# A batch-normalised matmul: one block's transposition moved from TensorE to the DMA, and the order of all tasks written down as a table

## The chip, the cores and the metric

The kernel runs on one core of a Trainium2 chip. The metric is the device time of one execution in microseconds (us), of which the median over runs is given. A trace of one profiled execution is used beside it. PE is TensorE, DVE is VectorE, ACT is ScalarE, POOL is GpSimd, SP is SyncE; on SP runs nothing but the issuing of DMAs.

## The reference

```python
y = np.matmul(x, weight)                 # x (16, 512, 1024), weight (1024, 768), float32
mean = np.mean(y, axis=(0, 1), keepdims=True)
var = np.var(y, axis=(0, 1), keepdims=True)
y_norm = (y - mean) / np.sqrt(var + eps)
return (gamma * y_norm + beta).astype(np.float32)
```

So y has 8192 rows and 768 columns, and every column is normalised over all 8192 rows. No output of a column can be written before the last row of that column has been multiplied.

## The kernel before

**Tiles.** The 768 columns are six column tiles `nt` of 128, the 8192 rows are sixteen chunks `c` of 512. x is loaded in bfloat16 by DMAs from GpSimd's queue, turned by VectorE so that the contraction lies on the partitions, and kept in SBUF. A unit of TensorE is one half of the contraction for one column tile and one chunk: four pairs of weight load and matmul with 512 moving columns (`col_unit`, line 575). Two such units fill one bank of PSUM; there are eight banks.

**Stages.** While x arrives, the first two column tiles are multiplied with rows on the partitions (line 510). Then column tiles 2, 3, 4 and 5 follow with columns on the partitions, so that a chunk's y is a block of 128 columns by 512 rows, transposed against the output. After each bank is full, VectorE takes its statistics (`bn`, line 711) and ScalarE copies it to SBUF as bfloat16 (`keep`, line 715); only then is the bank free. For column tile 2, ScalarE does both (lines 720 and 724). When a column tile is complete, `finish_tasks` makes its scale and shift.

**Output blocks.** Two chunks together are a block of 128 columns by 1024 rows (`col_block`). It is normalised in place (`norm`, lines 1023 and 1026) and must be transposed before it is stored. `MODE` on line 276 says how, for each block:

- `'xact'`: a transposing DMA on SP's queue (`xbar`, line 1220), then ScalarE's conversion to float32 (`convert`, line 1232), then the store (line 1202).
- `'pe'`: eight transpositions on TensorE into a PSUM bank (`turn_block`, line 1044), ScalarE's copy out of it (line 1210), then the store. The eight transpositions ride between the matmuls of later units, one after each matmul ("hosted").

Some blocks (`RAW`) are transposed by the DMA before they are normalised (line 1106), scaled by VectorE (line 1174) and shifted by GpSimd (line 1178); for these the scale and shift are spread over a PSUM tile by `raw_spread` (`turn` on lines 1141 and 1142, `gather` and `deal` on line 1145, on GpSimd or ScalarE, and ScalarE's copy on line 1158). The first two column tiles are normalised by VectorE (line 937) and shifted by GpSimd or VectorE (line 942).

**The end.** Column tile 5 is last. Two half blocks of column tile 4 are held back and copied out after the last matmul (line 1252). After the last statistics come ScalarE's square root (line 1311), three small instructions of VectorE (lines 1314, 1323, 1324), then norm (line 1348), transposition on TensorE (line 1044), ScalarE's copy (line 1361) and store (line 1364) for every block of the last column tile.

**The order.** Every step is a `Task` with a priority, an assumed duration and the tasks that it depends on. `arrange` goes through them in a planner's time, always takes the engine that can begin first and, on it, the task of lowest priority number among those that can begin within 0.2 us (`LOOK`); it also picks which TensorE unit hosts which transpositions and where buffers lie. Each engine then runs its instructions in exactly the order emitted, and waits on semaphores for what they need. VectorE tasks marked `lock` and GpSimd's arithmetic are not planned at the same time.

Of the kernel before, what the change touches and what calls it, by code (L numbers as in the profile page):

```python
# [97 lines left out]
class Wires:  # L98
# [8 lines left out]
    def ready(self, queue):  # L107
        lanes = self.lanes[queue]
        return 0.0 if len(lanes) < self.LANES else lanes[-self.LANES]
# [9 lines left out]
        return t, land  # L119


def arrange(tasks, turns, log=None):

    free = {e: 1.25 for e in ("PE", "DVE", "ACT", "POOL", "SP")}
    wires = Wires()
    port = {"DVE": 0.0, "POOL": 0.0}
    left = sorted(tasks, key=lambda t: t.prio)
    order = []  # L130
    SEM, LOOK = 0.06, 0.2

    def ready(t):
        if t.after is not None and t.after.end is None:
            return None
        r = 0.0
        for d in t.deps:
            if d.end is None:
                return None
            r = max(r, d.end + SEM + t.slack)  # L140
        kept = [(s.pool, s.pool.mark()) for s in t.takes] if len(t.takes) > 1 else []
        fits = True
        for s in t.takes:
            p = s.pool.place(s)
            if p is None:
                fits = False
                break
            r = max(r, p[0] + SEM)
            if kept:
                s.pool.take(s, p[1])  # L150
        for pool, mark in reversed(kept):
            pool.reset(mark)
        if not fits:
            return None
        if t.dma:
            r = max(r, wires.ready(list(t.engines)[0]))
        return r

    def start_of(t, r, e):

        b = max(r, free[e])
        if e == "DVE" and t.lock:
            b = max(b, port["POOL"])
        elif e == "POOL" and not t.dma:
            b = max(b, port["DVE"])
        return b

    while left:
        seen = [(t, ready(t)) for t in left]
        first = {}  # L170
        for t, r in seen:
            if r is not None:
                for e in t.engines:
                    b = start_of(t, r, e)
                    if e not in first or b < first[e]:
                        first[e] = b
        if not first:
            raise RuntimeError(f"nothing can begin: {[(t.prio, t.emit) for t in left[:8]]}")
        e = min(first, key=lambda k: first[k])
        best = None  # L180
        for t, r in seen:
            if r is not None and e in t.engines and start_of(t, r, e) <= first[e] + max(LOOK, t.look):
                if best is None or t.prio < best[1]:
                    best = start_of(t, r, e), t.prio, t
        start, _, t = best
        for s in t.takes:
            s.pool.take(s, s.pool.place(s)[1])
        occ, lat = t.engines[e]
        t.hosted = []
        if t.hosts:  # L190
            room = t.hosts
            for u, r in seen:
                if u in turns and r is not None and r <= start + 0.3 and room >= 1:
                    n = min(room, turns[u][0])
                    if turns[u][0] == turns[u][1]:
                        places = [s.pool.place(s) for s in u.takes]
                        if any(p is None or p[0] > start for p in places):
                            continue
                        for s in u.takes:
                            s.pool.take(s, s.pool.place(s)[1])  # L200
                        u.takes_done, u.takes = u.takes, []
                    t.hosted.append((u, n))
                    turns[u][0] -= n
                    room -= n
                    occ += 0.0555 * n
                    lat += 0.0555 * n
        if t in turns:
            occ = lat = 0.0555 * turns[t][0]
            lat += 0.2
            t.count = turns[t][0]  # L210
        free[e] = start + occ
        if e == "DVE" and t.lock or e == "POOL" and not t.dma:
            port[e] = start + occ
        t.end = start + lat
        if t.dma:
            free[e], t.end = wires.send(e, start, occ, t.dma, t.count)
        t.start, t.engine = start, e
        order.append(t)
        left.remove(t)
        for u, n in t.hosted:  # L220
            if turns[u][0] == 0:
                u.end = t.end + 0.2
                left.remove(u)
    return order


# [1 line left out]
def kernel(  # L228
# [9 lines left out]
    nc = tc.nc  # L238
# [3 lines left out]
    ALU = mybir.AluOpType  # L242
# [5 lines left out]
    P = 128  # L248
# [24 lines left out]
    XT, YB, SQ = C - EARLY, 28, 3  # L273
    ADDED = (0,6,16,28,40)
    PARTED, LATE, SINGLE = (4,5,7,8,9,10), (12,13,14,15), (2,3,6)
    MODE = {2:'xact',3:'xact',4:('pe',)*8}
    MODE = {nt: m if isinstance(m, tuple) else (m,) * (C // GY) for nt, m in MODE.items()}
    RAW, RAWADD, RAWDUE = {2:(0,2),3:(0,),4:(0,2,4)}, {2:'POOL',3:'POOL',4:'POOL'}, {2:14.0,3:8.0,4:8.0}
    RING = 3 * CH // 32 * KQ // 2
# [13 lines left out]
    def seq(bi):  # L293

        ins = bi.ins
        prev = last.get(ins.engine)
        if prev is not None:
            tc.add_manual_dep(
                ins, prev,
                mybir.DependencyInfo(mybir.DependencyClass.NoSync, mybir.DependencyReason.DATA),  # L300
                reason="order",
            )
        last[ins.engine] = ins.name
        return bi

    gamma_sb = singles.tile([P, NT], f32)
# [28 lines left out]
    ngamma = singles.tile([P, NT], f32)  # L335
# [29 lines left out]
    def act(occ):  # L365
        return {"ACT": (occ, occ + 0.11)}

    def pool(occ):
        return {"POOL": (occ, occ + 0.05)}
# [70 lines left out]
    order = [("x", 0), ("w", 0, 2), ("x", 1), ("w", 2, 4)]  # L440
# [5 lines left out]
    t = 1.0  # L446
    affine = None
# [237 lines left out]
    def y_of(nt, c):  # L685
        return y_col.setdefault((nt, c // GY), Slot(ys))
# [174 lines left out]
    S = clock[0]  # L861
# [61 lines left out]
    sr = task(U + 0.1, dve(0.35), shift_rows, [sc], True)  # L923
# [32 lines left out]
    k = 0  # L956
# [4 lines left out]


    def negate_gamma(eng):
        seq(nc.vector.tensor_scalar(ngamma, gamma_sb, -1.0, None, op0=ALU.mult))

    ng = task(S, dve(0.1), negate_gamma, [affine, sr], True)

    def finish_tasks(nt):
        deps = [col_end[nt, c][0] for c in range(C)]
# [49 lines left out]
    def norm(nt, c, n=1):  # L1019
        def emit(eng):  # L1020
            part = y(nt, c, n)
            if eng == "ACT":
                seq(nc.scalar.activation(
                    part, part, AF.Identity, bias=shift[:, nt:nt + 1], scale=scale[:, nt:nt + 1]))
            else:
                seq(nc.vector.tensor_scalar(
                    part, part, scale[:, nt:nt + 1], shift[:, nt:nt + 1],
                    op0=ALU.mult, op1=ALU.add))
        return emit
# [161 lines left out]
    def col_block(nt, c, due, fin_task, held=False):  # L1191
# [26 lines left out]
        def xbar(eng):  # L1218
# [49 lines left out]
    for nt in range(GA, NT - 1):  # L1268
# [10 lines left out]
        f = finish_tasks(nt)  # L1279
        start = clock[0] + 3.0  # L1280
# [58 lines left out]
    for c, r0, rows in ends:  # L1339
        due = E + 2.0 + 0.6 * c  # L1340
        n = max(rows // CH, 1)
# [13 lines left out]
        b, bank = turn_block(due + 0.6 * (n - 1), nt, m0, count, norms, [y_of(nt, c + i) for i in range(n)])  # L1355
# [7 lines left out]
        def store(eng, slot=slot, m0=m0, count=count):  # L1363
# [48 lines left out]
```

## Time and profile before

| What | Value |
|---|---|
| Median of 3 runs | 205.89 us (205.88 to 206.04) |
| Span of the profiled execution | 204.1 us (204.07) |
| What lies around the span, by the difference | 1.8 us |
| PE busy | 189.3 us, 93% |
| DVE, ACT, POOL busy | 159.3, 146.2, 124.1 us |
| Read from and written to HBM | 36.71 MB, 25.17 MB |

The profiled execution has no time of its own beside its span; the runs are 1.8 us longer than the span, and this difference is taken as constant. Busy time is counted between the first and the last instruction. A busy TensorE is not TensorE at its peak: matmuls are pipelined, and the mean of one instruction (371 ns for 512 columns) is longer than the distance from one to the next (0.216 us).

### The profile page before, as it was taken

How to read it: one execution, taken by the hardware profiler on the slowest of the kernel's cores; microseconds unless marked ns; L12 is line 12 of the kernel's file. 1: busy time of each engine (PE TensorE's matmuls, PEld its weight loads, DVE VectorE, ACT ScalarE, POOL GpSimd, SP SyncE). 2: the span in 40 equal slices, each digit the busy share in tenths (PEclk: the TensorE clock that was granted, in tenths of full speed). 3: DMA queues.
4: the chain of work that ended last, by engine and by line, in shares of the span. 5: the costliest groups of instructions: out<-in, count | busy, mean ns of one | idle time of the engine just before them, and what ended most of it. 6: DMA issues, size and time to landing. Idle time of an engine off the chain costs nothing.

```text
span 204.1 us, 3510 instructions
## 1 busy us (share of the span) xinstructions
PE 189.3 (93%) x1210; PEld 114.5 (56%) x1210; DVE 159.3 (78%) x250; ACT 146.2 (72%) x260; POOL 124.1 (61%) x150
## 2 busy tenths in 40 slices
PE   7969999999999999999999999999999999997900
PEld 3457554657488888777865444444444445544600
DVE  4031879999999999969989998987999878657900
ACT  2001461368989999899978766999998959956950
POOL 7776954877499989997403999389613312940000
PEclk9999999999999999999999999999999999999965
DMA  4999999999999999999686899899999999999998
GB/s 71 172 199 196 176 196 196 196 197 197 190 193 197 197 196 196 196 197 195 103 181 200 297 339 336 248 301 328 295 322 227 336 303 274 347 343 310 310 347 253
DMA packets 98562, 48.74 MB, mean 239 GB/s; under 512 B 24304, under 2 KB 98032, under 8 KB 98544
## 3 DMA queue, kind: packets, MB, share of 16 engines
q0 software_dynamic: 34624, 18.36, 65.5%
q1 hardware_dynamic: 63920, 30.16, 52.6%
q8 instruction: 9, 0.15, 0.3%
q14 instruction: 9, 0.07, 0.1%
HBM read 36.71 MB, written 25.17 MB: 303 GB/s over the span
## 4 chain that ended last, share of the span: by engine, by line
PE 86%; ACT 3%; DMA 3%; POOL 2%; issue 1%; ACTq 0%; DVE 0%; POOLq 0%
PE y_ps L575 54%; PE y_ps L510 24%; PE y_ps L814 4%; ACT o_sb L1361 3%; DMA ring<-in_x_dram 3%; PE o_ps L1044 1%; POOL ring L403 1%; POOL w_sb L387 1%; PE y_ps L753 1%; PE a_ps L903 1%; PE o_ps L1074 0%; ACTq L1407 0%; PE idle_ps L591 0%; PE tot_ps L871 0%; ACT ring L1252 0%
## 5 line engine op out<-in xcount | busy, mean ns | idle before, releaser
L575 PEld LDWEIGHTS <-w_sb 128*128 128x128 bf16 x520 | 50.3, 97 | 57.6
L575 PE MATMUL y_ps<-xT_sb,w_sb 128*128 128x512 bf16 (+1 forms) x272 | 59.3, 371 | 0.0
L575 PE MATMUL y_ps<-x_pl,w_sb 128*128 128x512 bf16 x248 | 57.4, 379 | 0.0
L403 POOL DMA_DIRECT2D ring<-in_x_dram x76 | 47.2, 626 | 14.4 <-DMA ring<-in_x_dram 5.5
L510 PE MATMUL y_ps<-w_sb,xT_sb 128*128 128x256 bf16 x448 | 50.6, 273 | 1.7 <-DMA ring<-in_x_dram 1.6
L510 PEld LDWEIGHTS <-xT_sb 128*128 128x128 bf16 x448 | 43.5, 98 | 9.4 <-DVE xT_sb L435 2.9
L435 DVE STREAM_TRANSPOSE xT_sb<-ring 128x1024 f32<-128x1024 f32 (+1 forms) x29 | 31.2, 1111 | 14.1 <-DMA ring<-in_x_dram 13.9
L711 DVE BATCH_NORM_STATS2 stats<-y_ps 128x6 f32<-128x512 f32 x46 | 30.9, 687 | 7.7 <-PE y_ps L575 7.2
L715 ACT CAST y_sb<-y_ps 128x512 bf16<-128x512 f32 x51 | 29.0, 593 | 10.4 <-DVE stats L711 6.3
L547 ACT COPY x_pl<-xT_sb 128x1024 bf16<-128x1024 bf16 x32 | 32.8, 1063 | 1.7 <-DVE xT_sb L435 1.7
L942 POOL TENSOR_TENSOR ring<-ring,sum 128x1024 f32<-128x1024 f32 (+1 forms) x11 | 23.8, 2188 | 14.9 <-ACT y_ps L724 10.9
L659 ACT ACTIVATE sq_sb<-y_ps 128x512 f32<-128x512 f32 x28 | 16.3, 610 | 16.2 <-PE y_ps L510 15.9
L666 POOL TENSOR_TENSOR sum<-sum,sq_sb 128x512 f32<-128x512 f32 x20 | 25.6, 1278 | 3.0 <-ACT sq_sb L659 1.7
L662 DVE TENSOR_TENSOR sum<-y_ps,sum 128x512 f32<-128x512 f32 x28 | 18.9, 675 | 6.3 <-ACT sq_sb L659 5.3
L672 ACT CAST y_sb<-y_ps 128x512 bf16<-128x512 f32 x28 | 16.3, 594 | 8.2 <-DVE sum L662 8.0
L1178 POOL TENSOR_TENSOR ring<-ring,sum 128x1024 f32<-128x1024 f32 x6 | 14.8, 2477 | 9.8 <-issue 8.5
L937 DVE TENSOR_TENSOR ring<-y_sb,a_ps 128x1024 f32<-128x1024 bf16 (+1 forms) x16 | 16.7, 1079 | 0.1
L1044 PE MATMUL o_ps<-ident,y_sb 128*128 128x128 bf16 x104 | 13.1, 221 | 1.6 <-DVE y_sb L1348 1.5
L1232 ACT CAST ring<-ring 128x1024 f32<-128x1024 bf16 x13 | 13.8, 1063 | 0.6 <-DMA ring<-y_sb 0.6
L1145 POOL COPY sum<-sum 32x256 f32<-32x256 f32 (+1 forms) x17 | 5.8, 340 | 13.4 <-DVE sum L1142 6.5
L428 DVE STREAM_TRANSPOSE xT_sb<-ring 128x2048 bf16<-128x2048 bf16 x6 | 13.5, 2290 | 0.1
L591 PE MATMUL idle_ps<-idle_sb 128*128 128x512 f32 x18 | 9.6, 688 | 1.5 <-DVE idle_sb L316 1.5
(104 smaller groups left out, 153.7 us busy)
## 6 DMA issues: line engine op xcount, KB each, us to landing
out_dram<-ring SPq DMA_DIRECT2D x37, 512.0 KB, 3.4
ring<-in_x_dram POOLq DMA_DIRECT2D x52, 256.0 KB, 8.8
out_dram<-o_sb SPq DMA_DIRECT2D x6, 512.0 KB, 4.7
ring<-in_x_dram POOLq DMA_DIRECT2D x16, 128.0 KB, 5.9
w_sb<-in_weight_dram POOLq DMA_DIRECT2D x8, 192.0 KB, 6.2
out_dram<-ring SPq DMA_DIRECT2D x6, 256.0 KB, 3.0
ring<-in_x_dram POOLq DMA_DIRECT2D x4, 192.0 KB, 7.8
out_dram<-o_sb SPq DMA_DIRECT2D x3, 256.0 KB, 2.5
```

Source lines behind the costliest of these rows:

```text
L403: bi = seq(nc.gpsimd.dma_start(x_bf[32 * i:32 * i + 32], src[:, :, KQ * i:KQ * (i + 1)]))
L435: seq(nc.vector.transpose(dst, src[:, :, jw0:jw1]))
L510: seq(nc.tensor.matmul(y_ps[:, s], x_of(c, jw, e, t * P, (t + 1) * P), w_sb[:, jw, e, 0:NA], start=(s == 0 and jw == 0 and e == 0), stop=( ...
L547: seq(nc.scalar.copy(dst, pairs) if eng == "ACT" else ENG[eng].tensor_copy(dst, pairs))
L575: seq(nc.tensor.matmul(y_ps, w_sb[:, jw, e, nt * P:(nt + 1) * P], moving(c, jw, e, q0 * QR, q1 * QR, parted), start=(jw == 0 and e == 0 an ...
L659: seq(nc.scalar.activation(sq_sb[:, 0:n], slot.tile[:, 0:n], AF.Square))
L662: seq(nc.vector.tensor_add(sum1, slot.tile[:, 0:n], sum1))
L666: seq(ENG[eng].tensor_add(acc, acc, state["sq"][:, 0:n]))
L711: seq(nc.vector.bn_stats(dst, slot.tile))
L715: seq(nc.scalar.copy(y(nt, c), slot.tile))
L937: seq(nc.vector.tensor_mul(slot.o, y_row[c].y[:, s0:s1], aff[0][:, None, :].to_broadcast([P, n, NA])))
L942: seq(ENG[eng].tensor_add(slot.o, slot.o, row[:, None, :].to_broadcast([P, n, NA])))
```

## The change

Three edits. `MODE` for column tile 4 gets `'xact'` for its fifth block (chunks 8 and 9) in place of `'pe'`. The negation of gamma goes from VectorE to GpSimd. And `arrange` no longer chooses: it walks a table, `ORDER`, of 783 words (786 tasks without the three that are wholly hosted), in which each word names the engine (P, V, A, G, S) and the number of the task in order of creation, and after a plus sign the hosted transpositions. The bookkeeping of times and buffers stays.

```diff
+ORDER = (
+    "G0 P59 G3 G8 A9 G4 G7 V1 V2 P60 G10 P61 P62 P63 P64 P65 V5 V6 P66 G12 P67 P68 P69 P70 P71 G14 P76 A72 "
...
+    "P637 P689 G546 V638 P677 P681 P690 P678 P673 P674 V641 S547 A642 A562 A631 A615 A639 V643 V691 V661 V644 "
+    "V657 V665 V669 V675 V679 S559 S569 S640 S563 G645 S662 G646 P682+666.1,658.3 P685+658.3,666.1 "
+    "P693+666.3,658.1 P686+658.1,666.2 P694+666.1 A692 A566 A570 A647 A663 A676 A680 V648 V687 V695 V683 S567 "
...
+    "A760 A770 S743 S766 S781 S776 S761 S785 S771 "
+)
-    left = sorted(tasks, key=lambda t: t.prio)
+    left = tasks
-    while left:
-        seen = [(t, ready(t)) for t in left]
-        ...
-        start, _, t = best
+    for word in ORDER.split():
+        word, _, riders = word.partition("+")
+        t, e = left[int(word[1:])], NAMES[word[0]]
+        r = ready(t)
+        if r is None:
+            raise RuntimeError(f"out of order: {word}")
+        start = start_of(t, r, e)
...
-    MODE = {2:'xact',3:'xact',4:('pe',)*8}
+    MODE = {2:'xact',3:'xact',4:('pe','pe','pe','pe','xact','pe','pe','pe')}
...
-        seq(nc.vector.tensor_scalar(ngamma, gamma_sb, -1.0, None, op0=ALU.mult))
-    ng = task(S, dve(0.1), negate_gamma, [affine, sr], True)
+        seq(nc.gpsimd.tensor_scalar(ngamma, gamma_sb, -1.0, None, op0=ALU.mult))
+    ng = task(S, pool(0.3), negate_gamma, [affine])
```

Built, the two programs issue the same instructions in the same order on every engine until the last two chunks of the first two column tiles are multiplied, about 95 us into the span. From there on the orders differ as follows.

- **TensorE**: the half units of column tiles 2 to 5 are shuffled among chunks, so that more banks are half full at a time. Eight transpositions are gone. Those of two blocks of column tile 4 (tasks 658 and 666) ride together, one to four to a unit, those of a third (670) in two portions later.
- **VectorE**: the table interleaves statistics, norms and copies otherwise; one of the sixteen copies of line 547 that both engines may do comes to it from ScalarE; the negation is gone. Of the first two column tiles' blocks, it begins with another half chunk (chunk 1 first).
- **ScalarE**: four of the six norms of column tile 2 follow one another directly. The third `gather` is gone from it. At the end the square root stands ahead of both held copies, and both are ahead of the first copy of the last column tile.
- **GpSimd**: the negation before its first line-942 task, and the third `gather`.
- **SP**: fourteen transposing DMAs of line 1220 in place of thirteen, three of column tiles 2 and 3 in a row at two places. At the end, the first piece stored has 256 rows, then come two of 512 and one of 1024 before the second one of 256; the last store is of 1024 rows and not of 512.

More of the change, by code (lines that the diff above doesn't have):

```diff
@@ L128, in arrange @@
     port = {"DVE": 0.0, "POOL": 0.0}
-    left = sorted(tasks, key=lambda t: t.prio)
+    left = tasks
     order = []
-    SEM, LOOK = 0.06, 0.2
+    SEM = 0.06
     def ready(t):
@@ L166, in start_of @@
         return b
-    while left:
-        seen = [(t, ready(t)) for t in left]
[L170 to L184, printed above, removed]
-        start, _, t = best
+    NAMES = {"P": "PE", "V": "DVE", "A": "ACT", "G": "POOL", "S": "SP"}
+    for word in ORDER.split():
[5 more added lines that the diff above has]
+        start = start_of(t, r, e)
         for s in t.takes:
@@ L189, in arrange @@
         t.hosted = []
[L190 to L206, printed above, removed]
+        for rider in riders.split(",") if riders else ():
+            i, n = rider.split(".")
+            u, n = left[int(i)], int(n)
+            if turns[u][0] == turns[u][1]:
+                for s in u.takes:
+                    s.pool.take(s, s.pool.place(s)[1])
+                u.takes_done, u.takes = u.takes, []
+            t.hosted.append((u, n))
+            turns[u][0] -= n
+            occ += 0.0555 * n
+            lat += 0.0555 * n
         if t in turns:
@@ L218, in arrange @@
         order.append(t)
-        left.remove(t)
         for u, n in t.hosted:
@@ L222, in arrange @@
                 u.end = t.end + 0.2
-                left.remove(u)
     return order
```

33 rows, old and new, of the table ORDER are left out of this document.

## The prediction

> **What bounds the kernel now.** First the page: busy time in slices, then the chain that ended last.
>
> ```profile
> PE   7969999999999999999999999999999999997900
> PEclk9999999999999999999999999999999999999965
> GB/s 71 172 199 196 176 196 196 196 197 197 190 193 197 197 196 196 196 197 195 103 181 200 297 339 336 248 301 328 295 322 227 336 303 274 347 343 310 310 347 253
> PE 86%; ACT 3%; DMA 3%; POOL 2%; issue 1%; ACTq 0%; DVE 0%; POOLq 0%
> ...
> 177.82 6.99 PE y_ps L575 x32
> 184.80 1.81 PE y_ps L753 x16
> ...
> 186.92 0.58 ACT ring L1252
> 187.51 0.20 ACT std L1311
> ...
> 188.59 0.54 PE o_ps L1044 x4
> ```
>
> TensorE has no gap from 25 us on until its last matmul ends at 184.80 + 1.81 = 186.62 us, at a full granted clock. No order can make it denser; only taking instructions away, or a new gap, moves that moment. After it the end is a chain of small steps, then output.
>
> Second, the DMA in stages, because the change adds a transfer (columns: window, its length, then busy time of PE, PEld, DVE, ACT, POOL, granted clock, DMA share, GB/s).
>
> ```profile
> 110.00:128.00 18.00, 18.00 (x88) 7.87 (x86) 16.89 (x20) 13.41 (x43) 16.72 (x8) 1.00 0.91 321
> 128.00:146.00 18.00, 18.00 (x84) 8.04 (x83) 15.89 (x23) 18.00 (x26) 14.00 (x12) 1.00 1.03 301
> 180.00:187.50 7.50, 7.06 (x47) 4.01 (x44) 4.36 (x11) 3.64 (x8) 2.05 (x1) 1.00 1.14 343
> 187.50:191.50 4.00, 2.87 (x33) 1.88 (x34) 3.76 (x14) 3.49 (x10) 0.00 (x0) 1.00 0.85 253
> 191.50:202.50 11.00, 2.59 (x33) 1.73 (x32) 2.14 (x7) 5.17 (x7) 0.00 (x0) 0.69 1.15 347
> 168.00:169.50 1.50, 1.50 (x10) 0.69 (x8) 1.47 (x7) 1.00 (x3) 0.00 (x0) 1.00 1.28 288
> ```
>
> The output goes at 347 GB/s when nothing else limits it, and it is at that rate for the last 11 us. It has one hole at the end: 4 us at 253 GB/s, worth 4 x (1 - 253/347) = 1.08 us. The last column tile is 8192 x 128 x 4 bytes = 4.19 MB, 12.1 us at 347 GB/s. So the end is: last matmul, 2.7 us to the first store (it is issued at 189.31 us), 12.1 us of output, and the landing.
>
> Third, what the moved block costs on each side.
>
> ```profile
> L1044 PE MATMUL o_ps<-ident,y_sb x56: 218/219/231, 169.2 to 190.0; 128*128 128x128 bf16 x56
> DMA to landing us min/median/max: 3.4/4.4/5.6
> L1232 ACT CAST ring<-ring 128x1024 f32<-128x1024 bf16 x13 | 13.8, 1063 | 0.6 <-DMA ring<-y_sb 0.6
> L1210 ACT CAST ring<-o_ps 128x1024 f32<-128x1024 bf16 x4 | 4.0, 1014 | 0.2 <-DMA out_dram<-ring 0.2
> 110.46 2.52 POOL L942 TENSOR_TENSOR ring<-ring,sum 128x512 f32<-128x512 f32 x2 [10.85 <-ACT y_ps L724]
> 131.19 4.70 POOL L942 TENSOR_TENSOR ring<-ring,sum 128x1024 f32<-128x1024 f32 x2 [3.54 <-DVE ring L937]
> ```
>
> The first is the transposition on TensorE, the second the time from issue to landing of the thirteen transposing DMAs of line 1220.
>
> **The change, part by part.** *Eight transpositions off TensorE.* A transposition lasts 219 ns but takes 0.06 us of the chain (it alternates with matmuls of 0.22 us there), so eight give 0.45 us: the last matmul ends at 186.17 us. ScalarE's part stays: 1.06 us for 1.01.
>
> *One transposing DMA more.* A block is 1024 x 128 x 2 bytes = 0.262 MB. In the window from 168.0 to 169.5 us, where transpositions fill the DMA, it moves 288 GB/s: 0.91 us. The upper bound is the median time of issue on SP, 1.70 us; the lower bound is the store rate, 0.76 us. I take 1.3, halfway between 0.91 and 1.70, because switching between stores and transpositions leaves dips. The Trainium skill has two figures, on "Advanced Engine Details and Errata", X-Bar Transpose (TRN2), that transposing DMAs run as fast as regular ones at 350 to 400 GB/s, and on "DMA: Bandwidth & Descriptors", Latency and other measured facts, 261 GB/s for a transposition that isn't contiguous. By the first the price would be an estimated 0.70 us, by the second 1.00; the trace's 288 GB/s lies between and nearer the second.
>
> This transfer falls at about 169 us. From 180 us on the DMA is at 343 of 347 GB/s, so it is not hidden beside anything there: it makes all later stores 1.3 us later, up to the hole at 187.5 us, which holds 1.08. If nothing else moved, the end would be 0.2 us later.
>
> *The order, early.* GpSimd starts its additions at 110.46 us, after VectorE's shift at 106.87 us and then two norms (0.73), the negation (0.16), a product (0.68), an addition (0.69), two norms (0.73), a product (0.68). In the table stand three norms (1.1) and one product (0.68): GpSimd can start at about 108.7, 1.8 us sooner, and its later wait of 3.54 us on line 937 shrinks too. The output of the first two column tiles then comes sooner, in stages that ran at 321 and 301 GB/s; the lead, up to 1.8 us, pays for the 1.3 of the transposition. The negation on GpSimd lies in its 10.85 us of idle time: nothing. The third gather costs ScalarE 1.00 us less and GpSimd about 0.9 more, off the path unless GpSimd's addition behind it is late.
>
> *The order, the end.* ScalarE's square root starts when the statistics are aggregated in both. But now both held copies (0.58 each) and both keeps (0.37) stand between it and the first output copy; before, one held copy was done ahead of it. Root 186.97, then at starting distances of about 0.5, 0.3, 0.5 and 0.3 us the first output copy starts at 188.75 in place of 188.91 - 0.45 = 188.46: it loses 0.28 us. Then come pieces of 256, 512, 512 and 1024 rows instead of 256, 256, 512 and 512. Two pieces of 0.131 MB took 0.88 us on SP, 298 GB/s, under the DMA's rate, so one of them less, and more queued behind it, closes part of the hole: between 0 and 1.08 us, I take 0.3, the lower part, since half of the hole lies before the first store.
>
> Sum against the profiled span of 204.07 us: -0.45 + 0.28 - 0.30 = -0.47, with the transposition paid by the early lead. With 1.82 us around the span as before, 205.89 - 0.47 = **205.4 us**.
>
> **The rivals.** *(1) TensorE runs into full banks.* This is the mechanism for a slower end. Before, in program order, a bank was used again 10.45 us (six units of 1.73) after its last matmul in most of column tiles 3 to 5. In the table many gaps are 2.6 to 5 us, and a drain takes 0.69 (statistics) + 0.59 (keep) and semaphores, 1.4 us at best, and waits for whatever stands ahead in ScalarE's queue. The tightest place is column tile 5: a bank with a `'pe'` block's transpositions is full at 174.5 us and wanted again at 177.2, if I count the table's units on from 109 us with 0.216 us a matmul (0.226 where a row's step is two). Ahead of its copy, ScalarE has the conversion of the new block (0.95), two keeps (0.5 each) and another block's copy (0.93); with its own 0.93 that is 3.8 us. The new block's norm ends at 168.55 (it stands behind statistics of a unit that ends at 167.4). With the median landing of 4.4 us the conversion begins at 173.0 and the bank is free at 176.8: 0.4 us to spare. From a landing of 4.8 us on TensorE waits, at the largest landing seen, 5.6, for 0.8 us; and VectorE waited up to 0.72 us for a store to free its buffer, which the old order hid. About eight places have 0.1 to 1.3 us to spare, and a stall at one gives slack to the next, so the largest counts: 0.8 to 2 us, time 206.2 to 207.4, say 206.9. For it: every conversion now stands close ahead of keeps. Against: laid out with the rows' durations, no place is late by itself.
>
> *(2) The DMA stays the bound.* If the early lead is lost (three transpositions in a row on SP, stores behind them), the 1.3 us remain, up to 1.70 and more with a pause: 0.2 to 0.6 us later than before, 206.2. For it: 343 GB/s before the end. Against: 2 us of room at 301 to 321 GB/s earlier.
>
> *(3) Nothing to see.* The gain of TensorE is eaten by ScalarE's order at the end: -0.45 + 0.28, 205.7. This is part of the forecast's own range, 205.1 to 205.8.
>
> **How the numbers follow.** What a measurement of this kernel can tell from no change is about 0.2%, 0.41 us. My case has a chance of 0.50, of which 0.37 lie below 205.48 and 0.13 within 0.2% (the forecast stands only just outside). Rival 1 has 0.37, all slower. Rival 2 has 0.13, 0.05 within 0.2% and 0.08 slower. That makes faster 0.37, same 0.18, slower 0.45. The range for 8 in 10 goes from 204.9 (the whole hole closed) to 207.1, leaving out the worst of rival 1.
>
> **What would show it.** Right: TensorE without gaps up to a last matmul at about 186.2 us; GpSimd's first line-942 task near 108.7; a first output store at about 189.1; more than 253 GB/s in the four us after 187.5. Wrong: waits of TensorE on ScalarE in lines 1210, 1232 or 715, as the waits of PE name them, above all between 125 and 145 and between 170 and 178 us (rival 1); a last matmul in time but 347 GB/s without a hole from 180 us to a later end (rival 2); conversions on ScalarE that wait for a landing longer than 4.8 us.

## The result, and the profile after

| | before | changed |
|---|---|---|
| Median of six runs | 205.94 us (205.65 to 206.11) | 206.93 us (206.64 to 207.98) |
| Ratio, 95% interval | | 1.0055 (1.0039 to 1.0071) |
| Span of the profiled execution | 204.07 us | 204.99 us |

The changed kernel is slower by about 1.0 us. Every line of the changed kernel stands 24 lines lower than before (575 is 599, 1044 is 1068, 1364 is 1388).

The page first: TensorE's and the clock's slices, the DMA's rate, the shares of the chain that ended last.

```profile
PE   7989999999999999999999999999999999996830
PEclk9999999999999999999999999999999999999575
GB/s 71 159 201 196 194 196 196 196 197 196 190 194 197 196 196 197 196 197 194 95 202 170 381 357 308 234 355 337 310 229 338 221 292 329 332 343 293 343 347 184
PE 79%; DMA 9%; DVE 3%; POOL 2%; ACT 1%; issue 1%; ACTq 0%; DVEq 0%; POOLq 0%
```

Two rows of the chain itself (start, length, engine, tile, line):

```profile
184.52 1.83 PE y_ps L777 x16
...
187.12 0.30 ACT std L1335
```

From 95 us on, where the orders begin to differ, TensorE has no new gap (ahead of that it stood for 0.13 us at 18.4 and 0.27 us at 25.8 us, waiting for data; the old order with six gamma loads, below, shows 0.28 us at 26.0 in the same place). Its last matmul ends at 184.52 + 1.83 = 186.35 us, 0.27 us sooner than before. So the loss lies behind it, or beside it. The DMA in stages (the columns as before, GB/s last):

```profile
110.00:128.00 18.00, 17.89 (x80) 7.79 (x81) 17.21 (x20) 15.07 (x50) 16.52 (x9) 1.00 0.97 342
128.00:146.00 18.00, 17.94 (x82) 8.02 (x83) 14.76 (x23) 15.43 (x21) 13.42 (x12) 1.00 1.12 308
146.00:165.00 19.00, 18.89 (x87) 8.51 (x88) 17.25 (x35) 16.61 (x25) 5.68 (x8) 1.00 1.10 271
165.00:180.00 15.00, 14.88 (x86) 7.42 (x87) 10.30 (x21) 11.85 (x18) 5.68 (x9) 1.00 1.17 322
180.00:187.50 7.50, 6.78 (x46) 3.96 (x44) 6.35 (x15) 4.53 (x9) 4.09 (x2) 1.00 1.13 340
187.50:191.50 4.00, 2.80 (x28) 1.90 (x28) 3.93 (x14) 3.86 (x9) 0.00 (x0) 0.83 0.93 281
191.50:202.50 11.00, 4.23 (x37) 3.67 (x36) 1.84 (x6) 5.36 (x6) 0.00 (x0) 0.66 1.15 347
```

The early stages run faster than before (342 for 321, 308 for 301), the hole before the end is smaller (281 for 253), and yet the end is later. From 146 to 165 us the rate is lower than before. The two stages of the kernel before that the prediction doesn't show:

```profile
146.00:165.00 19.00, 19.00 (x89) 8.58 (x88) 17.08 (x34) 16.47 (x25) 5.19 (x9) 1.00 1.19 288
165.00:180.00 15.00, 15.00 (x95) 7.73 (x93) 11.99 (x24) 13.11 (x22) 6.37 (x6) 1.00 1.12 320
```

The lead on GpSimd, the first output copy on ScalarE and the first output store on SP, from their timelines:

```profile
108.84 12.05 POOL L966 TENSOR_TENSOR ring<-ring,sum 128x512 f32<-128x512 f32 x6 [8.87 <-DVE ring L961]
```

```profile
188.79 2.57 ACT L1385 CAST o_sb<-o_ps 128x256 f32<-128x256 bf16 x5
```

```profile
189.22 10.15 SPq L1388 DMA_DIRECT2D out_dram<-o_sb  x11
```

**Three pieces make up the loss.** (1) The trace holds sixteen completion events for each store, which I read as one from each of the 16 DMA engines. In both kernels the last of the sixteen falls behind the other 15 after 180 us, and from then on the last completions of the stores follow one another at the time of their transfers (about 1.51 us for 512 KB, 0.76 for 256 KB, 0.38 for 128 KB) up to the end: that engine has no pause. From the completion events:

| | first output store issued | 15 engines done | last engine done |
|---|---|---|---|
| before | 189.31 | 203.13 | 203.15 |
| changed | 189.22 | 203.00 | 203.54 |

The 15 gained 0.13 us; the last landing is 0.39 later. Both figures contain 0.14 us that came from the start of this execution and not from the change: the last matmul of the first two column tiles, up to which the orders are the same, ended at 94.86 us in place of 94.72. Counted from that moment the profiles agree far better:

| us from the end of that matmul | last matmul | first output store | 15 engines done | last engine done |
|---|---|---|---|---|
| before | 91.90 | 94.60 | 108.41 | 108.44 |
| before, six loads (below) | 91.90 | 94.60 | 108.42 | 108.54 |
| changed | 91.47 | 94.36 | 108.15 | 108.68 |
| changed, four loads (below) | 91.47 | 94.36 | 108.15 | 108.64 |

So by the order TensorE is 0.43 us sooner, the 15 engines 0.27 sooner and the last engine 0.25 us later than in the first row.

(2) After it the program waits on SP for eight completion semaphores, one after another. The instructions of the program's last line from 203.1 us on (count, shortest, median and longest in ns, first and last start), before and changed:

```profile
L1407 SPq EVENT_SEMAPHORE  x3: 17/17/28, 203.2 to 204.0; - x3
...
L1407 ACTq DRAIN  x1: 14/14/14, 203.5 to 203.5; - x1
```

```profile
L1431 SPq EVENT_SEMAPHORE  x10: 17/28/28, 203.6 to 204.9; - x10
...
L1431 ACTq DRAIN  x1: 142/142/142, 204.6 to 204.6; - x1
```

Two of these belong to the last steps in both; so one wait came behind the last landing before, and eight do now, 0.06 us each: 0.43 us. SP's waits show the same from the other side (total, times, longest): before, SP still waited for landings three times, the longest 1.5 us; now it waits once for 4.1 us, on the first semaphore, and finds the other seven done.

```profile
SPq L1407 <- DMA out_dram<-o_sb: 2.8, 3, 1.5
```

```profile
SPq L1431 <- DMA out_dram<-o_sb: 4.1, 1, 4.1
```

(3) ScalarE's DRAIN takes 142 ns in place of 14, comes late and makes the last steps 0.10 us longer. It does so in every kernel below that has the whole table or all but its last entries, and in no other. In just these kernels an 8 KB packet of instructions stands 0.3 us behind the end of the span (205.30 us here), and in the others the last one comes before 192 us; whether that is the cause was not tried. 0.39 + 0.43 + 0.10 = 0.92 us, the difference of the spans, of which 0.14 is the start of the execution.

### The profile page after: what moved, and what is told of

The parts are those of the page before. It is cut to its first block, busy times and chain, and to the rows that moved or that the text cites. A ratio compares the mean times of both kernels' runs of the same rounds, so it can differ in the third digit from the quotient of the medians.

```text
span 205.0 us, 3478 instructions
## 1 busy us (share of the span) xinstructions
PE 190.3 (93%) x1188; PEld 116.2 (57%) x1202; DVE 158.9 (78%) x250; ACT 143.2 (70%) x255; POOL 126.9 (62%) x155
## 4 chain that ended last, share of the span: by engine, by line
PE 79%; DMA 9%; DVE 3%; POOL 2%; ACT 1%; issue 1%; ACTq 0%; DVEq 0%; POOLq 0%
PE y_ps L599 50%; PE y_ps L534 21%; DMA w_sb<-in_weight_dram 6%; PE y_ps L838 4%; DMA ring<-in_x_dram 3%; DVE y_sb L1372 2%; PE o_ps L1068 2%; ACT o_sb L1385 1%; POOL ring L427 1%; PE y_ps L777 1%; POOL w_sb L411 1%; DVE xT_sb L459 1%; PE a_ps L927 1%; PE o_ps L1098 0%; ACTq L1431 0%
## 5 line engine op out<-in xcount | busy, mean ns | idle before, releaser
L599 PE MATMUL y_ps<-xT_sb,w_sb 128*128 128x512 bf16 (+1 forms) x265 | 60.2, 371 | 0.3
L459 DVE STREAM_TRANSPOSE xT_sb<-ring 128x1024 f32<-128x1024 f32 (+1 forms) x29 | 31.3, 1112 | 13.8 <-DMA ring<-in_x_dram 13.6
L739 ACT CAST y_sb<-y_ps 128x512 bf16<-128x512 f32 x51 | 28.0, 589 | 10.3 <-DVE stats L735 7.7
L735 DVE BATCH_NORM_STATS2 stats<-y_ps 128x6 f32<-128x512 f32 x46 | 30.0, 685 | 6.4 <-PE y_ps L599 6.4
L571 ACT COPY x_pl<-xT_sb 128x1024 bf16<-128x1024 bf16 x31 | 31.8, 1053 | 1.7 <-DVE xT_sb L459 1.7
L696 ACT CAST y_sb<-y_ps 128x512 bf16<-128x512 f32 x28 | 16.0, 602 | 7.6 <-DVE sum L686 7.4
L1202 POOL TENSOR_TENSOR ring<-ring,sum 128x1024 f32<-128x1024 f32 x6 | 14.1, 2366 | 9.2 <-issue 5.6
L1169 POOL COPY sum<-sum 32x64 f32<-32x64 f32 (+1 forms) x21 | 8.6, 412 | 15.2 <-DVE sum L1166 14.4
L1256 ACT CAST ring<-ring 128x1024 f32<-128x1024 bf16 x14 | 14.4, 1045 | 0.5 <-DMA ring<-y_sb 0.4
L615 PE MATMUL idle_ps<-idle_sb 128*128 128x512 f32 x18 | 10.3, 727 | 1.5 <-DVE idle_sb L340 1.5
```

The costliest lines, as they stand in the source:

```text
L459: seq(nc.vector.transpose(dst, src[:, :, jw0:jw1]))
L571: seq(nc.scalar.copy(dst, pairs) if eng == "ACT" else ENG[eng].tensor_copy(dst, pairs))
L599: seq(nc.tensor.matmul(y_ps, w_sb[:, jw, e, nt * P:(nt + 1) * P], moving(c, jw, e, q0 * QR, q1 * QR, parted), start=(jw == 0 and e == 0 an ...
L735: seq(nc.vector.bn_stats(dst, slot.tile))
L739: seq(nc.scalar.copy(y(nt, c), slot.tile))
```

## The experiments

All ratios are to the kernel before on the same chip, with 95% intervals. What the expectations call a ring is one of the 16 DMA engines.

### The waits at the end

One gamma load less in the changed kernel, so that SP issues 88 DMAs again and not 89:

```diff
-    PAIRED = 1
+    PAIRED = 2
```

> The changed kernel with one DMA issue less on SP: gamma comes in four loads instead of five (two columns a load for the first four column tiles), 88 issues instead of 89, everything else as it is. Theory of the last waits: at the end SP waits for eight completion semaphores one after another in a fixed order at 0.06 us each, and with 89 issues the last store is on the first of the eight, so seven more waits follow its landing than before; with 88 the last store is on the last of the eight again, one wait follows, and the time falls by 7 x 0.06 = 0.43 us, to about 206.5 us, ratio to before 1.003. Theory that the whole loss is DMA work (one more transposition, a ring that lags): a load of 1 KB at the start changes nothing, 206.9 us, ratio 1.0055.

206.34 us, ratio 1.0029 (1.0012 to 1.0047): 0.6 us better than the changed kernel. The ten semaphore instructions at the end are three again:

```profile
L1431 SPq EVENT_SEMAPHORE  x3: 17/17/28, 203.8 to 204.7; - x3
...
L1431 ACTq DRAIN  x1: 141/141/141, 204.4 to 204.4; - x1
```

And one load more in the kernel before:

```diff
-    PAIRED = 1
+    PAIRED = 0
```

> The kernel before with one DMA issue more on SP: six gamma loads instead of five, 89 issues instead of 88, nothing else. Theory of the last waits: the last store moves to the semaphore that is waited for first, seven waits of 0.06 us come behind its landing, 0.43 us slower than before, ratio 1.002. Theory that the number of issues doesn't matter: ratio 1.000.

206.26 us, ratio 1.0029 (1.0014 to 1.0044), with the ten waits of the changed kernel:

```profile
L1407 SPq EVENT_SEMAPHORE  x10: 17/28/28, 203.6 to 204.9; - x10
```

Both directions agree, at sizes that hold 0.43 us. The number of DMA issues decides which of the eight semaphores the last store is on; one transposition more moved it from the last to the first. The late DRAIN of ScalarE stays with four loads: it goes with the table, not with the count.

### The transposition and the table

The kernel before, planned by itself, with the block moved:

```diff
-    MODE = {2:'xact',3:'xact',4:('pe',)*8}
+    MODE = {2:'xact',3:'xact',4:('pe','pe','pe','pe','xact','pe','pe','pe')}
-    PAIRED = 1
+    PAIRED = 2
```

> The kernel before, in its own planned order, with the one block of the fifth column tile turned by the DMA, and with four gamma loads so that the issues stay 88; no table, and the negation on VectorE. Theory that the transposition is what is paid for (0.91 to 1.3 us of DMA in a stage with no room): slower than before by 0.3 us or more, or no faster although the last matmul ends 0.3 to 0.45 us sooner. Theory that the table is at fault and the transposition is a gain: 0.3 us faster than before, ratio 0.9985 or less.

207.42 us, ratio 1.0075 (1.0059 to 1.0091): 1.5 us slower than before, with a last matmul at 186.36 us. The hole is gone:

```profile
187.50:191.50 4.00, 3.12 (x31) 2.62 (x32) 3.93 (x14) 3.28 (x7) 0.00 (x0) 0.76 1.14 341
```

So the transposition without the table costs 1.5 us, and the table gives 1.1 of it back (206.34 with the same count of issues). Which part of the table? The order of before up to about 153 us, and the new table's order from there:

```diff
-ORDER = "(the table's 783 words)"
+ORDER = "(610 words: the order of before, written out) (what is left of the table's words, in its order)"
-    PAIRED = 1
+    PAIRED = 2
```

> The other half: the order of the kernel before up to about 153 us (its first 610 tasks, the negation on VectorE), from there the table's order with the transposing DMA; four gamma loads, 88 issues. Theory that the table's early lead pays for the transposition: without it the loss of the planned order with the block moved comes back, ratio near 1.0075 (207.4 us). Theory that the table's late order is what helps (fewer stores that find the DMA empty at the end, three transpositions behind one another): ratio near that of the changed kernel with four gamma loads, 1.003 (206.3 us).

207.59 us, ratio 1.0081 (1.0060 to 1.0103): without the early lead the whole loss is back. The early part of the table is what pays. (The two orders fit less than perfectly here too: TensorE's last matmul came 92.40 us after those of the first two column tiles and not 91.47. But the end is later than this alone allows: first output store at 190.53 us, and 13.8 us behind it, by the bound found below, is 204.3; the last engine was done at 205.02.) Is the transposing DMA itself then still felt in the changed kernel?

```diff
-            seq(nc.sync.dma_start_transpose(t_slot.o, y(nt, c, GY)))
+            if nt != 4:
+                seq(nc.sync.dma_start_transpose(t_slot.o, y(nt, c, GY)))
...
-                seq(nc.scalar.copy(slot.o, t_slot.o))
+                src = t_slot.o if nt != 4 else y(nt, c, GY).rearrange("p (s n) -> p s n", n=P)
+                seq(nc.scalar.copy(slot.o, src))
```

> The changed kernel without its new transposing DMA: the conversion on ScalarE reads the block as VectorE wrote it, so that this block's output is not turned; TensorE doesn't turn it either; 88 issues with five gamma loads. What the DMA costs in the changed kernel, everything else as it is: compared with the changed kernel with four gamma loads (206.34 us, also 88 issues). Theory that the DMA bounds the end and the transposition is 0.91 to 1.3 us of it: faster by 0.4 to 1.0 us (the rest is hidden once the hole before the end opens again), 205.3 to 205.9 us, ratio to before 0.997 to 1.000. Theory that the early lead hides it wholly: no change, 206.3 us, ratio 1.002 to 1.003.

The kernel leaves this one block unturned. 206.47 us, ratio 1.0034 (1.0013 to 1.0055), no better than with it (1.0029). From 165 to 180 us the DMA moves 308 GB/s in place of 320: without the transfer it isn't filled. Last, the other half, with the block on TensorE:

```diff
-ORDER = "(the table's 783 words)"
+ORDER = "(the table's first 610 words) (what is left, in the order of before)"
-    MODE = {2:'xact',3:'xact',4:('pe','pe','pe','pe','xact','pe','pe','pe')}
+    MODE = {2:'xact',3:'xact',4:('pe',)*8}
```

> The table's order up to about 155 us (its first 610 entries), from there the order of the kernel before, written out as a table; the block stays on TensorE (no transposing DMA more, 88 issues). Theory that the table's early lead only pays for the transposition's DMA work: without that transposition the DMA has room anyway (hole of 1.08 us before the end), TensorE's last matmul and the first output store set the end as before, so the time is that of before, ratio 0.999 to 1.001. Theory that the early lead is worth something by itself: about 1.1 us faster than before, as the table is against the planned order with the block moved (206.34 against 207.42), ratio 0.995. Theory that the early part of the table is a loss: slower than 1.002.

209.77 us, ratio 1.0191 (1.0171 to 1.0210), slower by far more than any theory said. At the seam the two orders do not fit: a transposition (line 1127 there) stands on SP in front of stores that are ready, and waits 7.4 us for its input.

```profile
SPq L1127 <- ACT y_sb L736: 7.4, 1, 7.4
```

This run says nothing on what the lead is worth without the transposition. That stays open.

### The order at the end

Four loads, and the last words of the table (from its 713th) in the order of before:

```diff
-ORDER = "(the table's 783 words)"
+ORDER = "(the table's first 712 words) (what is left, in the order of before)"
```

> The changed kernel with four gamma loads whose last 71 entries stand in the order of the kernel before: output pieces of 256, 256, 512 and 512 rows, the second held copy and the second keep later on ScalarE. By the prediction's terms the old order wins 0.28 us for the first output copy and loses 0.3 us in the hole: no change within 0.1 us, 206.3 us, ratio 1.003. If the DMA alone bounds the end: no change either, but with an earlier first store (188.9 in place of 189.2 us). If the new order of the end is itself a loss: 0.3 us faster, ratio 1.0015; if it is a gain that was hidden: 0.3 us slower or more, ratio 1.0045.

206.51 us, ratio 1.0045 (1.0024 to 1.0065). The first store came at 189.64 us, not sooner: in the spliced order a keep and a held copy stood ahead of ScalarE's square root, which began at 187.72 us (187.37 with four loads alone). The lagging engine was then only 0.20 us behind at the end. The ratio is the one of the last theory, but against four loads alone (1.0029) it is no gain and no loss beyond the intervals: the run decides for none of them.

Four loads, and the second keep (A719) behind the first output copy (A738):

```diff
-A734 A719 S732 ... V772 V782 V778 ... P737 P745 ... A738 A746
+A734 S732 ... V772 P737 A738 A719 V782 V778 ... P745 ... A746
```

> The changed kernel with four gamma loads, and ScalarE's second keep of the last column piece (0.39 us, between the second held copy and the first output copy) moved behind the first output copy; nothing else. Theory that the first output store sets the end: it comes 0.17 to 0.28 us sooner (at about 0.3 us behind TensorE's transposition as before) and the time falls by as much, about 206.1 us, ratio 1.0015 to 1.002. Theory that the DMA ring that is behind by the instruction fetch sets the end (it has no idle time from 181.5 us on): an earlier first store with the same end, 206.3 us, ratio 1.003.

206.32 us, ratio 1.0019 (1.0007 to 1.0030); with four loads alone it was 206.34. From the last matmul to the first store it took 2.79 us in place of 2.87: the other work of the end left only 0.08 us to win, and one engine was still 0.52 us behind the 15 at the last landing. By the ratios (1.0019 against 1.0029, the intervals overlap) the run doesn't decide between the two theories.

### The lagging engine

Four loads, and in `wake`, which warms TensorE up before the first x lands:

```diff
-            for _ in range(count):
+            for _ in range(count - 3 if count == WAKE else count):
...
-            for _ in range(SMALL if count == WAKE else 0):
+            for _ in range(SMALL + 48 if count == WAKE else 0):
```

> The changed kernel with four gamma loads, and with three of the eight warm-up matmuls at the start replaced by 48 small ones (some 84 more instructions on TensorE, inside the time in which it waits for the first x; the warm-up's output is used nowhere). Theory of the lagging ring: a 16 KB instruction fetch for TensorE (every 256 of its instructions) puts one of the 16 DMA rings 1.4 to 1.7 us behind; in the changed kernel it falls at 181.5 us, after which the DMA has too little room to make it up, and 0.5 us of it is left at the last landing. With 84 more instructions at about 9 per us the fetch comes 9 us earlier, near 172 us, and is made up by 180 us: all 16 rings end together, 0.4 to 0.5 us sooner than with four loads alone, about 206.0 us, ratio to before 1.000. Theory that the ring's lag costs nothing: the same as with four loads alone, about 206.5 us.

209.07 us, ratio 1.0145 (1.0123 to 1.0167), a miss that shows two things. (TensorE also stood for 0.87 us at 18 us, so the warm-up did not leave the start as it was.) The 16 KB packet came at 176.0 us and a further one at 197.9, and in the profiled execution the last engine ended 1.44 us after the other 15 (206.31 against 204.87): a fetch shortly before the end is added to the end. And from 175.5 us, with a transposing DMA under way, nearly all traffic stopped for over 2 us. The DMA's rate from 175 to 178 us in 40 slices, and TensorE's and ScalarE's waits between 174 and 180 us:

```profile
GB/s 284 263 276 273 256 256 232 89 31 17 14 7 0 219 0 0 0 0 0 0 0 0 0 0 0 0 7 10 7 10 7 10 10 10 10 10 113 273 300 287
```

```profile
ACT ring L1234 <- DMA out_dram<-ring: 1.8, 1, 1.8
...
PE y_ps L599 <- ACT ring L1234: 1.0, 1, 1.0
```

The other direction, and its control in the kernel before (the same diff of the warm-up: 1 in place of 8 matmuls of 512 columns, 120 in place of 8 small ones):

> The changed kernel with four gamma loads, seven of the eight warm-up matmuls at the start replaced by 112 small ones (about 196 more instructions on TensorE before the first x lands; the warm-up's output is used nowhere). With a fetch every 256 instructions this puts each 16 KB fetch some 6.5 us later: the one at 181.5 comes at about 188, in the hole before the first output store, and none follows. Theory that the lagging ring is the last to end in the changed kernel: all 16 rings end together, 0.4 to 0.5 us sooner than with four gamma loads alone (206.34, ratio 1.003), so about 205.9 us, ratio 1.000 to 1.001. Theory that the first output store sets the end whatever the ring does: no change, ratio 1.003. What could spoil it: the fetch at 157 moves to about 163.5, before transpositions near 167 us; if they wait for the lagging ring and TensorE waits for them, the time is longer, 207 us or more.

> The same warm-up in the kernel before, as a control for what the warm-up itself does. There the ring that lagged from 182 us on has caught up by 192.6 us, so moving the fetch from 179.8 to about 186 us should change nothing if the start is not changed either: ratio 0.999 to 1.001. If the small matmuls at the start cost time (a colder clock, a later first matmul): slower by as much, and the run with the late fetch is to be compared with this one.

207.88 us, ratio 1.0098 (1.0083 to 1.0112), and 206.72 us, ratio 1.0036 (1.0014 to 1.0057). The control is slower too, with gaps on TensorE of 0.35 and 0.77 us near 16 us and later last matmuls (about 188 us), so the warm-up does not leave the start alone; the changed kernel also had TensorE wait 0.80 us for ScalarE at 146 us. Everything being late, the fetches (188.3 us, in the control 187.3) met the stores again. The times are inconclusive on the fetch. The completions of the control say more: with the fetch at 187.3 us its last engine ends 0.69 us after the 15 (205.54 against 204.85), where in the kernel before it was 0.02. (It is the profile of the slowest execution, 208.25 us.) In the changed kernel, whose lag lasts to the end either way, it is 0.46 and was 0.50. What the lag is worth was then asked by leaving out work of all 16 engines, in both kernels (in the kernel before with `PAIRED = 0`):

```diff
         def store(eng):
-            seq(ENG[eng].dma_start(dst(), slot.o))
+            if (nt, c) != (4, 12):
+                seq(ENG[eng].dma_start(dst(), slot.o))
```

> The changed kernel without one store of 512 KB, that of the block at x columns 12 and 13 of the fifth column tile (about 183 us; that part of the output is left unwritten), five gamma loads, so 88 issues and the last store on the semaphore that is waited for last. To be compared with the changed kernel with four gamma loads (206.34 us, also 88). Theory that one DMA ring, 1.2 to 1.5 us behind the others by TensorE's instruction fetch, works without a pause from 179 us to the end and sets it: this store is 1.51 us of its work, so it catches up in the pause before the first output store, all 16 rings end together and 13.8 us after that store's issue: 0.5 us sooner, 205.8 us, ratio 0.9995 to 1.001. Theory that all rings are bound by the amount of output: 1.5 us sooner, 204.8 us, ratio 0.995. Theory that TensorE and the first output store alone set the end: no change, 206.3 us, ratio 1.002 to 1.003.

> The same store left out of the kernel before (six gamma loads, 88 issues). There the ring that fetched has just caught up at the end (its last landing is 0.02 us after the others'), so both bounds stand at the same place: by the theory of the one ring taken together with the first output store, no gain, ratio 0.999 to 1.000. By the theory that the amount of output bounds all rings: 1.5 us faster, ratio 0.993.

The kernel before: 205.91 us, ratio 1.0003 (0.9989 to 1.0017): half a megabyte less to store, and nothing gained. The changed kernel: 206.20 us, ratio 1.0017 (0.9999 to 1.0035), lowest run 205.46 us against 205.97 with four loads and all stores; the medians differ by 0.14 us, within the intervals. The completions say it more clearly than the times:

| | first output store issued | 15 engines done | last engine done | first store to 15 done |
|---|---|---|---|---|
| before | 189.31 | 203.13 | 203.15 | 13.82 |
| before, a store less | 189.59 | 203.38 | 203.42 | 13.79 |
| changed | 189.22 | 203.00 | 203.54 | 13.78 |
| changed, four loads | 189.47 | 203.26 | 203.76 | 13.79 |
| changed, a store less | 190.51 | 204.27 | 204.30 | 13.76 |
| block moved, no table | 189.06 | 203.70 | 204.76 | 14.64 |

(The profiled execution of the changed kernel with a store less had a stall of 1.58 us on TensorE at 106 us, so its times stand later; its differences count. The stall held the output back as well, 321 GB/s from 110 to 128 us and 336 with four loads alone, so it gave the lagging engine little time of its own to catch up; one profile is all there is.) With the store left out, the last engine ends 0.03 us after the others and not 0.50. There are two bounds, then: first output store plus 13.8 us, and the engine that fetched, which works without a pause. Before, they stand within 0.02 us of each other (0.12 with six loads). In the changed kernel the second is 0.5 us later. That the gain is the whole 0.5 us in time was not resolved.

## Why the prediction was wrong

It forecast 205.4 us, 0.5 us faster; it became 206.93 us, 1.0 us slower. That lies in its range, on the side of its rivals. Point by point:

- **TensorE, -0.45 us: right.** The two profiles show -0.27, but executions of one order differ by 0.3 us, and they do so ahead of 95 us. From the last matmul of the first two column tiles to the very last it took 91.90 us in all three profiles of the old order with the block on TensorE (before, six loads, a store less) and 91.47 us in the changed kernel, with four loads and with the old tail: -0.43 us.
- **The early lead: right.** GpSimd began at 108.84 us (108.7 forecast). With the lead taken away the ratio was 1.0081 and not 1.0029, 1.1 us longer.
- **The transposition, 1.3 us, paid by the lead: right in effect.** 1.5 us where nothing pays for it, nothing that could be seen where the table does. Which price the transfer has by itself, the times do not tell; by the row of the trace it is 0.91 us at 288 GB/s. The Trainium skill ("Advanced Engine Details and Errata", X-Bar Transpose (TRN2)) has transposing DMAs as fast as regular ones, by which it would be an estimated 0.70 us. Here the trace doesn't agree, and it decides: transpositions stay at 288 GB/s beside stores at 347.
- **ScalarE's order, +0.28 us: right in kind.** Last matmul to first store took 2.87 us in place of 2.70: +0.17.
- **The hole, -0.30 us: this step failed.** The rate in it rose to 281 GB/s, by (281 - 253) x 4 / 347 = 0.32 us of output, as forecast. But that is no gain. Whatever moves in the hole, the first output store finds 15 engines waiting and they end 13.8 us after it, in both kernels: 13.78 in place of 13.82 is all that the larger pieces brought, 0.04 us of the 0.30. What stood in the hole was in part work from before it; the two held pieces, for one, went out at 187.91 us and not at 187.53. Without this term the sum was -0.17, the third rival's "nothing to see"; the 15 engines ended 0.13 us sooner, 0.27 without the late start of the execution.
- **The end as one number for 16 engines: the step that decided.** "Last matmul, 2.7 us to the first store, 12.1 us of output, and the landing" and the hole were read from a rate summed over 16 engines. The engine that fetches instructions at 181 us had no hole in either kernel. So there was no gain to be had from an earlier last matmul, and its own end moved by +0.39 us: 0.17 because the DMA stood that much further back at 179.4 us (0.14 of it from the start of the execution), 0.22 because the store over which the fetch fell took 3.04 us from one last completion to the next and not 2.82. Why it took longer there stays open; with four loads it is 3.04 again. This is the second rival, "the DMA stays the bound", in one engine; it had 0.2 to 0.6 us and a chance of 0.13. Its sign, 347 GB/s without a hole, was wrong for the same reason: the mean of 16 has a hole that the one has not.
- **The steps from the last landing to the end of the span, taken as constant: failed.** They have no term in the sum ("and the landing" ends it) and became +0.43 us for the semaphore of the last store and +0.10 for ScalarE, more than half of the loss. What lies around the span did stay: 206.77 - 204.99 = 1.78 us for 1.82. Counting SP's issues, 88 to 89, would have shown the first, if the order of the final waits had been read from the trace of before.
- **Rival 1, full banks: did not happen** in the changed kernel (no matmul of TensorE waits for ScalarE). Its mechanism is real: with the fetch moved, a late landing held ScalarE for 1.8 and TensorE for 1.0 us.

Where did the lead go? Against before, the DMA moved (342 - 321) x 18 = 378 and (308 - 301) x 18 = 126 KB more up to 146 us, and (271 - 288) x 19 = -323 KB from there to 165. The added transposition is 262 KB of what it moved, so with (322 - 320) x 15 = 30 more up to 180 us the output stood 51 KB behind, 0.15 us at 347 GB/s: the 0.17 above. The late start of the execution by itself makes 0.14 us x 347 GB/s = 49 KB, so the lead paid for the transposition, and nothing was left of it.

The place at which the DMA fell back most is that where SP issued three transposing DMAs directly one after another (148.50 to 152.45 us) and no store: from 150 to 155 us it moved 231 GB/s, and before 302, 348, 303, 335 and 324 in these five microseconds, 457 KB more. The rest of the stage made some of that good.

```profile
150.00:155.00 5.00, 5.00 (x24) 2.25 (x23) 4.97 (x13) 4.73 (x6) 2.11 (x5) 1.00 0.93 231
```

Both kernels also have a pause behind a fetch. The DMA from 158 to 164 us in the changed kernel, 0.15 us a slice, and the two microseconds of the kernel before from 156 us:

```profile
GB/s 331 318 352 324 348 355 341 352 348 338 365 323 289 294 288 79 20 24 20 24 20 20 19 82 251 290 269 290 292 285 96 297 283 259 278 276 271 283 276 236
```

```profile
156.00:157.00 1.00, 1.00 (x6) 0.45 (x5) 1.00 (x3) 1.00 (x2) 0.00 (x0) 1.00 1.67 33
157.00:158.00 1.00, 1.00 (x7) 0.44 (x5) 1.00 (x3) 0.40 (x2) 0.00 (x0) 1.00 0.62 134
```

In the changed kernel a fetch came at 157.1 us, one engine was 1.5 us behind at the landing of 160.2, and from there to 161.5 about 20 GB/s were left, what one engine of 16 moves (347 / 16 = 22). Before, the fetch came at 155.6 us and the pause from 156.0 to 157.4, so the pause is not what the kernels differ by. In both, and in the run with the early fetch, packets of a transposing DMA hang meanwhile: those of 256 bytes, 18 ns each otherwise, took up to 1.36, 1.50 and 2.29 us. That a transposition waits for the engine that is behind is read from this; it was not tried by itself, and in the run with the early fetch the pause began 0.5 us ahead of the 16 KB packet.

No version beat the kernel before: the best, with four loads and the later keep, is at 1.0019 of it.

## What to carry to other kernels

A rate over 16 DMA engines can show a hole that the slowest engine does not have: look at the spread of each transfer's sixteen completions before counting on the hole. Find each bound of the end separately (here first store plus a constant, and one engine's unbroken work); a term that improves only one of them, or that fills time ahead of the step that sets the end, is worth nothing. And count the DMA issues that a change adds: the semaphore on which the last one lands can cost as much as the change was to bring.

## What the runs showed of the hardware

- Instructions come in packets that take one DMA engine's time: those of 16 KB 0.88 to 1.78 us. That they are TensorE's is inferred: between two of them TensorE started some 250 matmuls and weight loads (258 from 157.1 to 181.5 us, 178 to 295 elsewhere in the changed kernel), and a longer warm-up moved them. While the DMA is full, the last completion of a store stays 1.3 to 1.7 us behind the middle one of the sixteen (182.1 to 189.5 us before, 184.0 to 189.9 us in the changed kernel, after fetches at 179.8 and 181.5), and the lag shrinks only in a pause. The last fetch came at 180.3 us with the block alone moved and at 181.5 us with the table as well. That it is the same engine throughout is inferred from the times; the trace does not name it.
- With a transposing DMA under way, nearly all traffic can stop around such a fetch: for 1.2 us at 160 us, 1.4 us at 156 us in the kernel before, and over 2 us in the run with the early fetch.
- The program's final waits cost 0.06 us for each semaphore behind the one that the last landing sets.
- Single executions are 1.1 to 1.4 us longer than the median, with the table (205.97 to 207.69 us with four loads) and without it (206.06 to 207.40 us with six loads). One profile shows a way: a fetch at 103.55 us, the third of three transpositions landing 1.5 us later, and TensorE without work for 1.58 us.
